# Linear attention's key transposes follow the values, empty steps between the gate pieces, and output tails at fixed steps of the last gate job and the first output job

## The chip, the cores and the metric

The program runs on one core of one Trainium2 chip. A run's time is device time in microseconds; the time of a kernel is the median of its runs. The engines of a core are PE (TensorE), DVE (VectorE), ACT (ScalarE), POOL (GpSimd) and SP (SyncE, which issues the weight transfers here). Each works through its own instructions in a fixed order, and waits where an operand or a buffer is not ready.

## The reference

Two layers of a 1024-wide hybrid block run over a sequence of 16 meta tokens and 512 frames (L = 528), followed by a second block of another kind, which the change does not touch. In each of the first block's layers one wide projection gives the inputs of two attentions: gated linear attention (4 heads) and forgetting attention (8 heads, softmax with a decay). Their normed and gated outputs lie side by side in `mix`, which the output projection multiplies. For the linear attention, cut to what the change touches:

```
log_b = cumsum(log_a)                       # per chunk of 64 frames, and for the meta tokens
u[c]  = sum_s (k_s * exp(log_end - log_b_s)) v_s^T
S_c   = exp(log_end) * S_{c-1} + u[c];   o_t = q_t^T S_c
mix   = concat(rms_norm(o) * silu(gate), fox) ;  h = h + mix @ w_out
```

Decays come from a low-rank projection (`sm`), through a log-sigmoid and a cumulative sum along the tokens.

## The kernel before

Activations stand transposed, 128 features on the partitions and 528 tokens along the row, each as a pair of rounded high and low halves. A projection onto 128 features is a job: 8 contraction tiles, for each of them three products (high by high, low by high, high by low) in two halves of 264 columns, so 48 matmuls on line 321 into a PSUM tile `mm`, of which there are two. When a job ends, DVE takes its `mm` tile out with a multiply by the row norm (`scaled`, L377, or L379 with a factor more); the next job but one cannot start before that. The weights of a job are split ahead of it: ACT rounds (`wh`, L272), DVE subtracts (`wl`, L273).

The order of jobs in a layer is a list: sm, gk0, gk1 (linear keys), fk0, fq0, fv0 (forgetting attention's first pair of heads: keys, queries, values), fk1, fq1, fv1, gv0, gv1 (linear values), then pairs 2 and 3 with gv2, gv3, gq0, gq1, then gr0 to gr3 (output gates), then 8 output jobs out0 to out7.

Everything that isn't a job is cut into pieces and put into a queue (`push`); while a job runs, after each of its 8 contraction tiles the queue hands out pieces at a rate (`pump`), a rate of 1.3 a step in the first jobs. A job can also carry pieces at fixed steps (`at`), and `flush` empties the queue before a job. A scheduler then sets the order on each engine; evacuations go with high priority, and `pin` holds an instruction to its place in the written order.

The pieces that the change concerns:

- `gates` (L383 on): the log-sigmoid of the decays, a scan along the tokens for the forgetting gate (`fox`, L417) and two sets of nine scans for the linear decays (`scan(0)`, `scan(1)`, L431), each followed on POOL by a subtraction (L434), on ACT by an exponential into `e` (L442) and small ones into `dec` (L449).
- `gla_k`: multiplies a key tile by `e` (L689), transposes it on PE (L693, L704) into PSUM tiles `to_tokensT`, of which there are two, and copies it out (L174, L176, L705) into zeroed tiles (L697). `gla_states` reads these much later, after gv3.
- `gla_v`: the same for the values (L462, L465).
- `fox_prep` (L519): transposes of fv0 as soon as it is out; `fox_k` (L492 to L494) and `stack_q` (L503) make high and low halves of keys and queries, the low ones on line 179.
- `gla_tail`: transposes of one head's normed output (L823, L827), two multiplies by gain and gate on DVE (L828), rounding on ACT (L829) and the low half on DVE (L179). It fills `mix[h]`. `st["scale"]` holds the multiplies by the head norm (L761) that go ahead of it.

In the kernel before, `gla_k` of a tile is pushed when that key job is taken out, and the tails of heads 0 and 1 and the scale pieces of heads 2 and 3 go through the queue when gr0 and gr1 are taken out; tails 2 and 3 stand at steps 2 and 4 of out0. The output jobs read `mix` in the order 4, 5, 6, 7, 0, 1, 2, 3.

Of the kernel before, what the change touches and what calls it, by code (L numbers as in the profile page):

```python
# [12 lines left out]
ALU = mybir.AluOpType  # L13
# [14 lines left out]
FULL = [(0, 264), (264, 264)]  # L28
# [8 lines left out]
class Net:  # L37
# [352 lines left out]
    def gates(self, i, sm, st):  # L390


        nc = self.nc
        R = slice(32, 40)
        ts, mzs = [self.G() for _ in range(3)], [self.G() for _ in range(3)]
        lbs, es, z = [], [], {}
        rows = [R, slice(0, 128), slice(0, 128)]

        def pre(m):
            bias = self.vec("ba", 2 * i + m)  # L400
            for a, n in ((0, HALF), (HALF, L - HALF)):
                ps = self.PS("gla_gateS_")
                nc.tensor.matmul(ps[:, :n], lhsT=self.wa[:, i, 128 * m:128 * m + 128], rhs=sm[:, a:a + n],
                                 start=True, stop=True)
                self.log_sigmoid_parts(ps[:, :n], bias, mzs[1 + m][:, a:a + n], ts[1 + m][:, a:a + n])

        def exps():
            for t, r in zip(ts, rows):
                nc.scalar.activation(t[r, :], t[r, :], AF.Exp, scale=-1.0)

        def logs():
            for t, r in zip(ts, rows):
                self.pin(nc.scalar.activation(t[r, :], t[r, :], AF.Ln, bias=1.0))

        def fox():
            c, z["r"] = self.G(), self.G()
            nc.vector.tensor_tensor_scan(c[R, :], mzs[0][R, :], ts[0][R, :], 0.0, op0=ALU.add, op1=ALU.subtract)  # L417
            nc.scalar.activation(self.c3[R, :], c[R, :], AF.Copy)
            nc.gpsimd.tensor_tensor(z["r"][R, :], c[R, :], self.c3[R, :], op=ALU.subtract)

        def fox_rest():
            r = z["r"]
            c2 = self.slots.tile([128, L], BF16, tag="g", name=self.n("g"))
            self.pin(nc.scalar.activation(c2[R, :], r[R, :], AF.Copy))
            self.pin(nc.scalar.activation(self.c3[0:8, :], r[R, :], AF.Copy))
            nc.gpsimd.tensor_tensor(self.c3[64:72, :], r[R, :], c2[R, :], op=ALU.subtract)

        def scan(m):
            lb, e, t, mz = self.G(), self.G(), ts[1 + m], mzs[1 + m]
            for a, n in [(0, META)] + [(META + 64 * c, 64) for c in range(8)]:  # L430
                nc.vector.tensor_tensor_scan(lb[:, a:a + n], mz[:, a:a + n], t[:, a:a + n], 0.0,  # L431
                                             op0=ALU.add, op1=ALU.subtract)
            lv = lb[:, META:].rearrange("p (c t) -> p c t", t=64)
            nc.gpsimd.tensor_tensor(e[:, META:].rearrange("p (c t) -> p c t", t=64), lv,  # L434
                                    lv[:, :, 63:64].to_broadcast([128, 8, 64]), op=ALU.subtract)
            nc.vector.tensor_scalar(e[:, :META], lb[:, :META], lb[:, META - 1:META], None, op0=ALU.subtract)
            lbs.append(lv)
            es.append(e)

        def decays():  # L440
            for m in range(2):
                nc.scalar.activation(es[m], es[m], AF.Exp, scale=-1.0 / 16)  # L442
                st["e"].append(es[m])
                for b in range(2):

                    dec = self.small.tile([128, 16], F32, tag=f"dec{2 * m + b}", bufs=2, name=self.n("dec"))
                    lv = lbs[m][64 * b:64 * b + 64].rearrange("p (j e) t -> p j e t", e=2)
                    for e in range(2):
                        nc.scalar.activation(dec[64 - 64 * e:128 - 64 * e, :4].unsqueeze(2), lv[:, :, e, 63:64],  # L449
                                             AF.Exp, scale=1.0 / 16)  # L450
                    st["dec"].append(dec)

        self.log_sigmoid_parts(sm[R, :], self.bf[R, i:i + 1], mzs[0][R, :], ts[0][R, :])
        return [lambda: pre(0), lambda: pre(1), exps, logs, fox, lambda: scan(0), lambda: scan(1), fox_rest, decays]

    def to_tokens(self, src, dst, dmeta, mcol, eng):

# [380 lines left out]
    def layer(self, i):  # L838
        nc, a = self.nc, self.a
        w_in = a["w_in"][i]  # L840
        st = dict(e=[], dec=[], kt=[], gvt=[], S={}, S0={}, om={}, on={}, gr={}, gk={}, gq={}, gv={}, scale={})
        fst = [dict() for _ in range(4)]
        mix = [None] * 8
# [27 lines left out]
        def ev_fk(p):  # L871
            return lambda ps: self.fox_k(fst[p], self.scaled(ps, FULL, self.rs))

        def ev_fq(p):
            def f(ps):
                t = self.scaled(ps, FULL, self.rs, extra=0.125)
                fst[p]["q"] = [self.stack_q(t, b) for b in range(2)]
            return f

        def ev_fv(p):  # L880
            def f(ps):
                fst[p]["fv"] = self.scaled(ps, FULL, self.rs)
                self.fox_pair(fst[p], i, p, mix, p == 3)
            return f

        def ev_gk(m):
            def f(ps):
                t = self.scaled(ps, FULL, self.rs)
                self.push(lambda: self.gla_k(st, m, t))
            return f  # L890

        def ev_gv(h):
            def f(ps):
                t = self.scaled(ps, FULL, self.rs)
                self.push(lambda: self.gla_v(st, h, t))
                if h == 3:
                    self.gla_states(st, 0)
                    self.gla_states(st, 1)
            return f
# [11 lines left out]
        def ev_gr(h):  # L911
            def f(ps):
                t = self.scaled(ps, FULL, self.rs)
                nc.scalar.activation(t, t, AF.Silu)
                tail = lambda: self.gla_tail(st, i, h, t, mix)
                if h == 0:
                    self.push(tail, *st["scale"][1])
                elif h == 1:
                    self.push(tail)
                else:  # L920
                    first_out["at"] = {**first_out.get("at", {}), 2 * h - 2: [tail]}
            return f

        rest = [(256, ev_gk(0)), (384, ev_gk(1))]
# [3 lines left out]
        for p in range(4):  # L928
            fox = [(2064 + 128 * p, ev_fk(p)), (1552 + 128 * p, ev_fq(p)), (2576 + 128 * p, ev_fv(p))]
# [9 lines left out]
                self.jobs[-2]["rate"] = 1.3  # L939

        self.norm_at(first, sums, spread)


        nxt = {}

        def ev_out(k):
            def f(ps):
                h = self.h[k]
                nc.vector.tensor_tensor(self.v(h, TO), self.psv(ps, TO), self.v(h, TO), op=ALU.add)
                if k == 0:  # L950
                    nxt["hs"] = []
                    nxt["acc"] = self.G()
                    if t0:
                        nc.gpsimd.memset(nxt["acc"][:, :t0], 1.0)
                nxt["hs"].append(self.hs_of(h[:, t0:], self.vec("ffn", 8 * i + k), None, t0, L))
                self.sq_acc(nxt["acc"], h[:, t0:], k == 0, 1.0, t0, L)
            return f
# [4 lines left out]
        for k in range(KT):  # L962
            if k % 2 == 0:
                ch = self.chunk([(self.wcols(w_out, 128 * k, 256), 0)], KT)
            self.job(ch, 128 * (k % 2), lambda: mix, TO, ev_out(k))
            if k == 0:
                first_out = self.jobs[-1]
            self.jobs[-1]["order"] = [4, 5, 6, 7, 0, 1, 2, 3]
            self.jobs[-1]["flush"] = k == 0

# [700 lines left out]
```

## Time and profile before

| | us |
|---|---|
| median of 3 runs | 2352.11 (2351.21 to 2354.13) |
| the profiled execution | 2356.24 |
| its span in the trace | 2354.5 |
| PE busy | 2316.9 (98% of the span) |
| DVE, ACT, POOL busy | 1369.2, 952.6, 251.8 (58%, 40%, 11%) |
| mean granted TensorE clock | 0.993 of full |
| chain that ended last, PE's share | 67% |

PE is busy nearly all the time, so what other engines do shows in the time only where PE stands, or where it runs at the lower of its two clocks. A row of the timeline gives the start, the duration, the engine, the line, the operation with output and input tiles, how many instructions of the kind were put together, and in brackets the idle time just before and what ended it.

### The profile page before, as it was taken

The page shows a single profiled execution, that of the slowest core. Times are in us where ns is not written, and L with a number is a line of the kernel's source. Part 1 is how long each engine was busy: PE and PEld are TensorE (multiplying, and loading weights), DVE is VectorE, ACT ScalarE, POOL GpSimd, SP SyncE. Part 2 cuts the span into 40 slices and gives each one's busy share as a digit, 9 for nine tenths or more (in the row PEclk, how much of TensorE's full clock was granted, in tenths as well). Part 3 has the DMA queues.
Part 4 walks back from the last instruction along what each step waited for, and adds up shares of the span by engine and source line. Part 5 has one row for each costly group of instructions (what it writes and reads, how often), then busy time and mean ns, then how long its engine had stood idle before and what let it go on. Part 6 is the DMA issues. An engine that isn't in the chain of part 4 may idle for free.

```text
span 2354.5 us, 37601 instructions
## 1 busy us (share of the span) xinstructions
PE 2316.9 (98%) x15703; PEld 2133.4 (91%) x15703; DVE 1369.2 (58%) x2445; ACT 952.6 (40%) x1641; POOL 251.8 (11%) x261
## 2 busy tenths in 40 slices
PE   7999999999999999999999999999999999999998
PEld 6999999999998998999998889988999888888888
DVE  6767556465556677466464666796454454333335
ACT  6565434233346655343242544322233533222225
POOL 3111210000022112200000131100000002101012
PEclk9999999999999999999999999999999999999999
DMA  4211122222332211222223222222212222332323
GB/s 115 73 55 55 55 90 90 90 90 88 96 87 55 55 55 55 90 91 90 90 84 106 82 80 87 90 90 90 90 54 72 72 90 90 95 102 90 99 85 130
DMA packets 217072, 196.77 MB, mean 84 GB/s; under 512 B 8987, under 2 KB 214791, under 8 KB 216903
## 3 DMA queue, kind: packets, MB, share of 16 engines
q1 hardware_dynamic: 216903, 194.37, 26.6%
q8 instruction: 124, 2.03, 0.3%
q14 instruction: 45, 0.37, 0.0%
HBM read 192.26 MB, written 2.10 MB: 83 GB/s over the span
## 4 chain that ended last, share of the span: by engine, by line
PE 67%; ACT 1%; DVE 1%; issue 1%; POOL 0%; DMA 0%; POOLq 0%; ACTq 0%; SPq 0%; DVEq 0%
PE mm L321 60%; PE valuesT L1157 1%; PE scoresS L1140 1%; PE foxV L619 1%; PE attend_pT L479 1%; PE foxT L599 0%; PE foxS L509 0%; ACT wh L272 0%; PE foxS L510 0%; PE spreadS L221 0%; DMA raw<-in_w_down_dram 0%; PE idx L509 0%; PE to_tokensT L462 0%; PE idx L510 0%; DVE g L431 0%
## 5 line engine op out<-in xcount | busy, mean ns | idle before, releaser
L321 PE MATMUL mm<-g,wh 128*128 128x264 f32 (+3 forms) x9168 | 1882.6, 316 | 9.5 <-DVE g L377 7.0
L321 PEld LDWEIGHTS mm<-g,wh 128*128 128x128 f32 x9168 | 1393.1, 190 | 109.0 <-issue 8.0
L321 PE MATMUL mm<-g,wl 128*128 128x264 f32 (+3 forms) x4552 | 1160.5, 313 | 0.0
L321 PEld LDWEIGHTS mm<-g,wl 128*128 128x128 f32 x4552 | 753.5, 190 | 49.6
L272 ACT ACTIVATE wh<-raw 128x1024 fp32r<-128x1024 f32 (+1 forms) x369 | 385.0, 1044 | 944.8 <-PE mm L321 800.6
L273 DVE TENSOR_TENSOR wl<-raw,wh 128x1024 fp32r<-128x1024 f32 (+1 forms) x369 | 444.1, 1204 | 74.8 <-ACT wh L272 65.9
L377 DVE TENSOR_TENSOR g<-mm,g 128x528 f32<-128x528 f32 (+2 forms) x228 | 158.5, 696 | 322.0 <-PE mm L321 317.3
L204 POOL TENSOR_TENSOR g<-g,g 128x528 f32<-128x528 f32 (+3 forms) x49 | 71.2, 1465 | 914.6 <-ACT g L203 568.1
L179 DVE TENSOR_TENSOR g<-g,g 128x512 fp32r<-128x512 f32 (+3 forms) x131 | 92.4, 706 | 38.4 <-ACT g L1009 29.2
L1034 DVE TENSOR_TENSOR g<-mm,g 128x528 f32<-128x528 f32 (+1 forms) x48 | 33.6, 700 | 119.1 <-PE mm L321 119.0
L991 ACT ACTIVATE g<-g,cv 128x528 f32<-128x528 f32 (+1 forms) x88 | 72.1, 819 | 17.7 <-DVE g L377 17.5
L1420 POOL TENSOR_TENSOR g<-g,g 128x512 f32<-128x512 f32 x22 | 38.9, 1767 | 281.9 <-ACT g L1419 281.9
L994 DVE SCALAR_TENSOR_TENSOR g<-g,cv,g 128x526 f32<-128x526 f32 (+1 forms) x88 | 66.8, 760 | 3.1
L993 DVE SCALAR_TENSOR_TENSOR g<-g,cv,g 128x527 f32<-128x527 f32 (+1 forms) x88 | 66.3, 754 | 1.8 <-ACT g L991 1.8
L179 DVE TENSOR_TENSOR g<-foxT,g 128x128 fp32r<-128x128 f32 (+1 forms) x160 | 50.5, 340 | 20.5 <-ACT g L604 18.2
L1005 ACT ACTIVATE g<-g 128x528 f32<-128x528 f32 (+1 forms) x44 | 28.1, 639 | 83.7 <-DVE g L994 83.7
L1007 DVE TENSOR_TENSOR g<-g,g 128x528 f32<-128x528 f32 (+1 forms) x44 | 30.8, 701 | 32.4 <-ACT g L1005 32.4
L187 POOL TENSOR_TENSOR sm<-sm,mhalf 128x10 f32<-128x10 f32 (+3 forms) x29 | 37.2, 1291 | 115.7 <-DVE sm L186 115.4
L574 ACT ACTIVATE g<-g,sm 128x144 f32<-128x144 f32 (+2 forms) x80 | 43.0, 538 | 16.0 <-DVE sm L570 15.3
L604 ACT ACTIVATE g<-foxT 128x256 fp32r<-128x256 f32 (+1 forms) x96 | 33.2, 346 | 27.9 <-PE foxT L599 21.8
L1009 ACT ACTIVATE g<-g 128x528 fp32r<-128x528 f32 (+1 forms) x44 | 28.1, 639 | 33.1 <-DVE g L1007 33.1
L1451 DVE TENSOR_TENSOR g<-mm,g 128x512 f32<-128x512 f32 x16 | 11.1, 692 | 50.0 <-PE mm L321 50.0
(282 smaller groups left out, 1696.4 us busy)
## 6 DMA issues: line engine op xcount, KB each, us to landing
raw<-in_w_up_dram SPq DMA_DIRECT2D x50, 1024.0 KB
raw<-in_w_in_dram SPq DMA_DIRECT2D x44, 1024.0 KB
raw<-in_w_down_dram SPq DMA_DIRECT2D x28, 896.0 KB
raw<-in_w_in_dram SPq DMA_DIRECT2D x28, 512.0 KB
raw<-in_w_out_dram SPq DMA_DIRECT2D x12, 1024.0 KB
raw<-in_w_down_dram SPq DMA_DIRECT2D x12, 1024.0 KB
raw<-in_w_gate_dram SPq DMA_DIRECT2D x10, 1024.0 KB
raw<-in_w_up_dram SPq DMA_DIRECT2D x10, 512.0 KB
```

What stands on the lines that cost most here:

```text
L179: (eng or self.nc.vector).tensor_tensor(out, x, hi.bitcast(F32), op=ALU.subtract)
L187: self.nc.gpsimd.tensor_tensor(out, v[:rows, :n], self.mhalf[:rows, :n], op=ALU.pow)
L204: nc.gpsimd.tensor_tensor(acc[:, t0:t1], tmp[:, t0:t1], acc[:, t0:t1], op=ALU.add)
L272: keep(nc.scalar.activation(hi[:, :K], src, AF.Copy))
L273: keep(nc.vector.tensor_tensor(lo[:, :K], src, hi[:, :K].bitcast(F32), op=ALU.subtract))
L321: nc.tensor.matmul(ps[:, b, :n], lhsT=w[:, k, :], rhs=x[:, t:t + n], start=(ki == 0 and pi == 0), stop=(ki == len(order) - 1 and pi == len ...
L377: self.nc.vector.tensor_tensor(self.v(out, toks), self.psv(ps, toks), self.v(rs, toks), op=ALU.mult)
L574: nc.scalar.activation(P[:qs, :N], P[:qs, :N], AF.Exp, scale=-1.0, bias=m, accum_out=col)
L991: nc.scalar.activation(A[:, lo:], U[:, lo:], AF.Identity, bias=self.vec("cb", 44 * i + t), scale=cw(2))
L993: nc.vector.scalar_tensor_tensor(A[:, s1:], U[:, s1 - 1:L - 1], cw(1), A[:, s1:], op0=ALU.mult, op1=ALU.add)
L994: nc.vector.scalar_tensor_tensor(A[:, s0:], U[:, s0 - 2:L - 2], cw(0), A[:, s0:], op0=ALU.mult, op1=ALU.add)
L1420: nc.gpsimd.tensor_tensor(z[:, META:], z[:, META:], self.rs[:, META:], op=ALU.mult)
```

## The change

Four things move; no arithmetic is added or taken away.

1. The transposes of the linear keys (`gla_k`) are pushed just ahead of those of the values with the same number, when gv0 and gv1 are taken out, and no longer when gk0 and gk1 are.
2. `gates` returns its pieces with empty steps between them (seven gaps), so that the queue hands out a scan later and spread out.
3. All the scans are pinned.
4. Tail 0 stands at step 1 of the last gate job (gr3), the two scale pieces at its steps 3 and 5, and tails 1, 2, 3 at steps 0, 2, 4 of out0.

```diff
@@ gates: scans
-            nc.vector.tensor_tensor_scan(c[R, :], mzs[0][R, :], ts[0][R, :], 0.0, op0=ALU.add, op1=ALU.subtract)
+            self.pin(nc.vector.tensor_tensor_scan(c[R, :], mzs[0][R, :], ts[0][R, :], 0.0, op0=ALU.add,
+                                                  op1=ALU.subtract))
...
-        return [lambda: pre(0), lambda: pre(1), exps, logs, fox, lambda: scan(0), lambda: scan(1), fox_rest, decays]
+        gap = lambda: None
+        return [lambda: pre(0), lambda: pre(1), exps, logs] + [gap] * 2 + [
+            fox, gap, lambda: scan(0), gap, gap, lambda: scan(1), gap, fox_rest, decays]
@@ layer: keys and values
         def ev_gk(m):
             def f(ps):
+                st["gk"][m] = self.scaled(ps, FULL, self.rs)
+            return f
+
+        def ev_gv(h):
+            def f(ps):
                 t = self.scaled(ps, FULL, self.rs)
-                self.push(lambda: self.gla_k(st, m, t))
-            return f
...
+                if h < 2:
+                    self.push(lambda: self.gla_k(st, h, st["gk"][h]))
                 self.push(lambda: self.gla_v(st, h, t))
@@ layer: gates of the output
                 nc.scalar.activation(t, t, AF.Silu)
-                tail = lambda: self.gla_tail(st, i, h, t, mix)
-                if h == 0:
-                    self.push(tail, *st["scale"][1])
-                elif h == 1:
-                    self.push(tail)
-                else:
-                    first_out["at"] = {**first_out.get("at", {}), 2 * h - 2: [tail]}
+                st["gr"][h] = t
...
+        tail = lambda h: lambda: self.gla_tail(st, i, h, st["gr"][h], mix)
+        scale = lambda x: lambda: st["scale"][1][x]()
+        self.jobs[-1]["at"] = {1: [tail(0)], 3: [scale(0)], 5: [scale(1)]}
...
             if k == 0:
-                first_out = self.jobs[-1]
+                self.jobs[-1]["at"] = {0: [tail(1)], 2: [tail(2)], 4: [tail(3)]}
```

In the changed file the lines behind `gates` stand three further down: the scan is L432, the multiply of a key L692, its transposes L696 and L707, a tail's multiplies L831.

**DVE in layer 0, behind the forgetting gate's scan.** Before, behind the first nine scans (g_449 is the key tile gk0, mm_466 is gk1's result, mm_612 fk0's):

```order
L431 SCALAR_TENSOR_TENSOR g_524<-g_445,g_442 128x64 x8
L436 TENSOR_SCALAR g_525<-g_524 128x16
L431 SCALAR_TENSOR_TENSOR g_543<-g_446,g_443 128x16
L431 SCALAR_TENSOR_TENSOR g_543<-g_446,g_443 128x64 x8
L436 TENSOR_SCALAR g_544<-g_543 128x16
L689 TENSOR_TENSOR g_449<-g_449,g_525 128x528
L273 TENSOR_TENSOR wl_609<-raw_451,wh_608 128x1024
L377 TENSOR_TENSOR g_603<-mm_466,g_381 128x528
L176 COPY g_592<-to_tokensT_587 64x4x64
L705 COPY km<-to_tokensT_600 16x2x64
L377 TENSOR_TENSOR g_678<-mm_612,g_381 128x528
L689 TENSOR_TENSOR g_603<-g_603,g_544 128x528
```

Of the change, from the end of the second nine scans to the evacuation of fv0 (mm_564 is fk0's result, mm_662 fq0's, mm_725 fv0's):

```order
L437 TENSOR_SCALAR g_578<-g_577 128x16
L692 TENSOR_TENSOR g_449<-g_449,g_537 128x528
L377 TENSOR_TENSOR g_644<-mm_564,g_381 128x528
L692 TENSOR_TENSOR g_555<-g_555,g_578 128x528
L179 TENSOR_TENSOR g_647<-g_644,g_646 64x528
L179 TENSOR_TENSOR g_653<-g_644,g_652 64x528
L273 TENSOR_TENSOR wl_659<-raw_451,wh_658 128x1024
L379 SCALAR_TENSOR_TENSOR g_711<-mm_662,g_381 128x528
L273 TENSOR_TENSOR wl_722<-raw_557,wh_721 128x1024
L179 TENSOR_TENSOR g_713<-g_711,g_713 64x528
L179 TENSOR_TENSOR g_716<-g_711,g_716 64x528
L377 TENSOR_TENSOR g_774<-mm_725,g_381 128x528
```

Ahead of that piece, between the two sets of scans, the change has gk1's evacuation (L377) and a weight split (L273). The copies L176 and L705 of the keys are gone from here; the multiplies of the keys by `e` have stayed.

**DVE around the first output job of layer 0.** Before, from the last weight split ahead of gr3 on (mm_3342 is gr2's result; the first L828 pair is tail 0's, the second tail 1's):

```order
L273 TENSOR_TENSOR wl_3442<-raw_2972,wh_3441 128x1024
L828 SCALAR_TENSOR_TENSOR g_3379<-gla_tailT_3380,cv,g_3170 128x272
L828 SCALAR_TENSOR_TENSOR g_3379<-gla_tailT_3385,cv,g_3170 128x256
L179 TENSOR_TENSOR g_3378<-g_3379,g_3377 128x528
L761 TENSOR_TENSOR g_3285<-g_3285,sm_3288 128x512
L761 TENSOR_TENSOR g_3315<-g_3315,sm_3318 128x512
L761 TENSOR_TENSOR om_3276<-om_3276,sm_3327 128x256
L828 SCALAR_TENSOR_TENSOR g_3408<-gla_tailT_3409,cv,g_3333 128x272
L828 SCALAR_TENSOR_TENSOR g_3408<-gla_tailT_3414,cv,g_3333 128x256
L273 TENSOR_TENSOR wl_3500<-raw_3336,wh_3499 128x1024
L179 TENSOR_TENSOR g_3407<-g_3408,g_3406 128x528
L377 TENSOR_TENSOR g_3438<-mm_3342,g_381 128x528
```

Of the change, from gr2's evacuation (mm_3342) on; mm_3414 is gr3's result, and L831 is tail 0 here:

```order
L377 TENSOR_TENSOR g_3407<-mm_3342,g_381 128x528
L186 TENSOR_SCALAR sm_3330<-sm_3326 128x2
L182 SCALAR_TENSOR_TENSOR g_3359<-foxN_3366,cv,g_3358 128x256
L273 TENSOR_TENSOR wl_3411<-raw_2972,wh_3410 128x1024
L831 SCALAR_TENSOR_TENSOR g_3423<-gla_tailT_3424,cv,g_3170 128x272
L831 SCALAR_TENSOR_TENSOR g_3423<-gla_tailT_3429,cv,g_3170 128x256
L179 TENSOR_TENSOR g_3422<-g_3423,g_3421 128x528
L764 TENSOR_TENSOR g_3285<-g_3285,sm_3288 128x512
L764 TENSOR_TENSOR g_3315<-g_3315,sm_3318 128x512
L377 TENSOR_TENSOR g_3480<-mm_3414,g_381 128x528
L764 TENSOR_TENSOR om_3276<-om_3276,sm_3327 128x256
L273 TENSOR_TENSOR wl_3486<-raw_3336,wh_3485 128x1024
```

gr2's evacuation has gone from behind tail 1 to ahead of tail 0. gr3's, which before came next to it, stands ahead of tail 1, whose three instructions follow directly behind the last row shown, in out0.

**PE in layer 0, in the job behind gv1, where values are transposed.** Before (g_1444 and g_1590 are the value tiles, mm_1802 the running job):

```order
L462 MATMUL to_tokensT_1765<-ident,g_1444 128x128 x4
L321 MATMUL mm_1802<-g_209,wl_1447 128x264
L321 MATMUL mm_1802<-g_226,wh_1446 128x264 x2
L321 MATMUL mm_1802<-g_227,wh_1446 128x264 x2
L321 MATMUL mm_1802<-g_226,wl_1447 128x264
L465 MATMUL to_tokensT_1771<-ident,g_1444 16x128
L462 MATMUL to_tokensT_1775<-ident,g_1590 128x128 x4
L465 MATMUL to_tokensT_1781<-ident,g_1590 16x128
```

Of the change (g_449 is the key tile gk0, g_1410 the first value tile, mm_1775 the running job):

```order
L696 MATMUL to_tokensT_1731<-ident,g_449 128x128 x4
L321 MATMUL mm_1775<-g_209,wl_1413 128x264
L321 MATMUL mm_1775<-g_226,wh_1412 128x264 x2
L321 MATMUL mm_1775<-g_227,wh_1412 128x264 x2
L321 MATMUL mm_1775<-g_226,wl_1413 128x264
L707 MATMUL to_tokensT_1744<-ident,g_449 16x128
L321 MATMUL mm_1775<-g_226,wl_1413 128x264
L321 MATMUL mm_1775<-g_244,wh_1412 128x264 x2
L321 MATMUL mm_1775<-g_245,wh_1412 128x264
L465 MATMUL to_tokensT_1748<-ident,g_1410 128x128 x4
L321 MATMUL mm_1775<-g_245,wh_1412 128x264
L468 MATMUL to_tokensT_1754<-ident,g_1410 16x128
```

Ahead of the values of head 0 now stand the five transposes of gk0, and behind these rows follow those of gk1 and of the second value tile in the same way. Before, the ten of the keys stood inside fk0 and fq0.

## Rows read from the trace of the kernel before

**Rows 1.** The page's first part: busy time and share of the span.

```profile
PE 2316.9 (98%) x15703; PEld 2133.4 (91%) x15703; DVE 1369.2 (58%) x2445; ACT 952.6 (40%) x1641; POOL 251.8 (11%) x261
```

**Rows 2.** Waits: engine and line, waited for; total us, times, longest.

```profile
PE to_tokensT L693 <- DVE g L689: 7.5, 3, 3.8
...
PE mm L321 <- DVE g L377: 7.0, 2, 3.5
```

**Rows 3.** Windows: us, busy (instructions) of PE, PEld, DVE, ACT, POOL; granted clock, DMA, GB/s.

```profile
50.20:56.90 6.70, 5.56 (x26) 5.49 (x27) 5.06 (x11) 4.88 (x12) 6.07 (x7) 0.50 0.00 0
...
57.10:63.80 6.70, 6.70 (x57) 6.68 (x57) 5.65 (x9) 3.53 (x7) 3.92 (x10) 1.00 0.42 128
...
130.00:140.00 10.00, 10.00 (x84) 9.75 (x83) 6.16 (x11) 6.95 (x12) 0.00 (x0) 1.00 0.41 107
...
258.50:265.10 6.60, 5.96 (x27) 6.00 (x28) 2.63 (x5) 1.90 (x3) 0.00 (x0) 0.50 0.01 2
...
729.50:732.70 3.20, 3.00 (x14) 2.69 (x13) 1.22 (x4) 2.12 (x7) 3.06 (x6) 0.50 0.00 0
...
937.70:940.90 3.20, 3.20 (x17) 3.20 (x16) 0.44 (x2) 0.61 (x1) 0.00 (x0) 0.50 0.00 0
```

**Rows 4.** Timeline of layer 0, from the start of fk0 to fq0.

```profile
43.03 0.64 PE L321 MATMUL mm<-g,wh 128*128 128x264 f32 x4
...
45.46 2.61 DVE L431 TENSOR_TENSOR_SCAN g<-g,g 128x16 f32<-128x16 f32 x9
...
48.12 2.44 DVE L431 TENSOR_TENSOR_SCAN g<-g,g 128x16 f32<-128x16 f32 x9
...
48.22 1.09 POOL L434 TENSOR_TENSOR g<-g 128x512 f32<-128x512 f32 x1 [0.84 <-DVE g L436]
...
50.63 2.69 POOL L434 TENSOR_TENSOR g<-g 128x512 f32<-128x512 f32 x1 [1.32 <-DVE g L431]
...
51.21 1.21 DVE L273 TENSOR_TENSOR wl<-raw,wh 128x1024 fp32r<-128x1024 f32 x1
...
51.34 1.12 PE L693 MATMUL to_tokensT<-ident,g 128*128 128x128 f32 x4 [3.75 <-DVE g L689]
...
53.36 0.64 ACT L442 ACTIVATE g<-g 128x528 f32<-128x528 f32 x1 [1.21 <-POOL g L434]
...
53.91 0.41 ACT L449 ACTIVATE dec<-g 64x4 f32<-64x4 f32 x2
...
54.91 1.06 ACT L272 ACTIVATE wh<-raw 128x1024 fp32r<-128x1024 f32 x1 [0.32 <-PE mm L321]
...
56.14 0.63 ACT L493 ACTIVATE g<-g 64x528 fp32r<-64x528 f32 x1
```

**Rows 5.** Timeline of layer 0: PE's first instructions of fk1, and fv0's transposes.

```profile
68.22 0.64 PE L321 MATMUL mm<-g,wh 128*128 128x264 f32 x4
...
69.19 0.65 PE L519 MATMUL foxV<-ident,g 128*128 128x128 f32 x4
```

**Rows 6.** Timeline of layer 0, around the start of out0.

```profile
251.14 0.88 DVE L828 SCALAR_TENSOR_TENSOR g<-gla_tailT,cv,g 128x272 f32<-128x272 f32 x2
...
257.67 0.70 DVE L179 TENSOR_TENSOR g<-g,g 128x528 fp32r<-128x528 f32 x1
...
258.29 1.31 DVE L377 TENSOR_TENSOR g<-mm,g 128x528 f32<-128x528 f32 x2
...
259.13 1.22 PE L321 MATMUL mm<-g,wh 128*128 128x264 f32 x4 [3.49 <-DVE g L377]
```

**Rows 7.** Timeline of layer 1: fk0's start, and the second scans.

```profile
722.32 0.73 PE L321 MATMUL mm<-g,wh 128*128 128x264 f32 x4 [0.33 <-DVE g L431]
...
724.73 2.44 DVE L431 TENSOR_TENSOR_SCAN g<-g,g 128x16 f32<-128x16 f32 x9
```

**Rows 8.** Timeline of DVE: the evacuations of out0 and out1 in layer 0.

```profile
269.12 0.71 DVE L949 TENSOR_TENSOR g<-mm,g 128x528 f32<-128x528 f32 x1 [0.85 <-PE mm L321]
...
274.96 0.71 DVE L949 TENSOR_TENSOR g<-mm,g 128x528 f32<-128x528 f32 x1 [3.03 <-PE mm L321]
```

More of the change, by code (lines that the diff above doesn't have):

```diff
@@ L430, in scan @@
             for a, n in [(0, META)] + [(META + 64 * c, 64) for c in range(8)]:
-                nc.vector.tensor_tensor_scan(lb[:, a:a + n], mz[:, a:a + n], t[:, a:a + n], 0.0,
-                                             op0=ALU.add, op1=ALU.subtract)
+                self.pin(nc.vector.tensor_tensor_scan(lb[:, a:a + n], mz[:, a:a + n], t[:, a:a + n], 0.0,
+                                                      op0=ALU.add, op1=ALU.subtract))
             lv = lb[:, META:].rearrange("p (c t) -> p c t", t=64)
@@ L887, in f @@
             def f(ps):
-                t = self.scaled(ps, FULL, self.rs)
-                self.push(lambda: self.gla_k(st, m, t))
+                st["gk"][m] = self.scaled(ps, FULL, self.rs)
             return f
```

## The prediction

> **What bounds the kernel now.** I read the page's busy times first: PE is busy for 98% of the span [rows 1]. So only two things can give time back: stretches in which PE stands, and stretches in which it runs at half clock. The list of waits comes next. Of PE's waits, two belong to code that the change touches [rows 2]: the key transposes (L693) waited three times for the multiply by `e` (L689), 7.5 us together, and a job's first matmul (L321) waited twice for an evacuation (L377), 7.0 us together. The timeline tells where. In layer 0 PE stands for 3.75 us at 51.34 until the key tile is multiplied [rows 4], and for 3.49 us at 259.13, where out0 starts, until gr2's `mm` tile is taken out [rows 6]. Layer 1 repeats both: 3.49 at out0, and 7.5 - 3.75 = 3.75 at its two key tiles. One small wait is added there, 0.33 us at 722.32 when fk0 wants its buffer [rows 7]. Together: 3.75 + 3.49 + 3.49 + 3.75 + 0.33 = 14.8 us of standing.
>
> The windows show the rest. From 50.2 to 56.9 the granted clock is 0.50 (1.2 GHz) and PE finishes 26 matmuls; in the 6.7 us behind it, at 1.00 (2.4 GHz), 57, so 0.1175 us each [rows 3]. At full clock 26 would take 3.05; PE was busy 5.56, so 2.5 us were lost to the clock. The stretch at out0 of layer 0 (5.96 busy, 27 matmuls) lost 2.8 by the same sum, those of layer 1 (3.00 busy with 14, 3.20 with 17) 1.35 and 1.2. Each of the four comes right behind one of the long waits, so I count them to the waits: 7.9 us. All that could be removed is 14.8 + 7.9 = 22.7 us.
>
> **The change, part by part.**
>
> *Output tails.* gr2's evacuation waited on DVE behind tail 1, whose two multiplies (0.88 for both) waited for PE transposes, and behind a weight split and a subtraction (0.70) [rows 6]. In the new order it stands ahead of tail 0, and gr3's ahead of tail 1. gr2's result is ready one whole job, 5.84 us (274.96 - 269.12, [rows 8]), before out0 wants the buffer, and only L182, a split and tail 0 lie around it. So both 3.49 go, with the clock losses 2.8 and 1.2: 11.0 us for both layers. What comes in is tail 1 in out0 beside tails 2 and 3. Each needs 0.88 + 0.70 us of DVE and a rounding on ACT of a tile like the one of 0.64 [rows 4] between them, 2.2 us in a row. Tail 3 starts at step 4 of 8, and contraction tile 3 comes last, at step 7, which is 3 x 0.73 = 2.2 us later. That is just enough when DVE is free, and DVE also has a split of 1.21 [rows 4] to do there. In the new order out1's first matmuls are mixed with out0's last 12, which covers most of a delay. I put 0.3 us a layer, between 0 and 1.5 (a split in front of the chain and 0.3).
>
> *The gates and keys of layer 0.* PE no longer transposes a key inside fk0, so the 3.75 and the 2.5 behind it go. The multiplies by `e` stay early on DVE, though, and with them the whole train behind the scans. I replay it from [rows 4] (jobs take 5.84, [rows 8]):
> - fk0 starts at 43.03, fq0 at 48.87, fv0 at 54.71, fk1 at 60.55. The first scans end at 48.07; gk1's evacuation follows at once (0.66, half of the pair at 258.29, [rows 6]), by 48.8, just in time for fq0.
> - A split (1.21) then goes ahead of the second scans (2.44), which end at 52.4 instead of 50.56.
> - POOL's subtraction for the second `e` follows. It took 1.09 beside scans and 2.69 beside a multiply, a split and an evacuation, 2.6 us of DVE work. Now only a multiply and an evacuation lie beside it: I take 1.75, with 2.69 as the upper end. It ends at 54.1, the exponential (0.64) at 54.8.
> - Behind that exponential on ACT stand the four copies of fk0's tile (0.63 each, to 57.3), two small exponentials (0.41) and the weight rounding (1.06), to 58.8. DVE's split waits for it: 60.0. Then in DVE's order: fq0's evacuation (0.66), a split (1.2), two subtractions (0.7 each, overlapping a little) and fv0's evacuation (0.66), to 63.8.
>
> Late next are the transposes of fv0. They stand 0.97 us into fk1 (69.19 against 68.22, [rows 5]), that is at 61.5; fv0's tile is there at 63.8. **So a new wait of 2.3 us comes in layer 0**, part of it perhaps 0.1 to 0.3 earlier, where fk1 wants fq0's buffer. With 2.69 for POOL everything is 0.94 later: 3.2. If the scheduler's train runs one split faster, 1.1; to 0 if ACT's four copies do not hold the rounding back. I take 2.3 and keep 0 to 3.5. The Trainium skill's "SBUF — State Buffer" (section "Who interferes with whom") says that a DVE instruction with two SBUF inputs contends with a GpSimd instruction that reads SBUF, and one with at most one SBUF input, as an evacuation has, does not. By that rule only the multiply would hold POOL, which gives 1.75 and the 2.3; by the row's full 2.69 the wait would be 3.2.
>
> A wait of 3.10 was followed by a half clock of 3.2 us that cost 1.35, one of 0.33 by none of its own [rows 2, 3, 7]. For 2.3 I take one such stretch, 1.3 us, between 0 and the 2.5 of [rows 3].
>
> *The same in layer 1.* All of 3.75 + 0.33 and the 1.35 go. Here gk0's evacuation is now ahead of the scans and both sets of scans stand ahead of gk1's. The second set started at 724.73 and took 2.44 [rows 7]; without the evacuation ahead of it (0.66) it ends at 726.5. Then a split (1.21) and gk1's evacuation (0.66): 728.4. fk0 started at 722.32 - 0.33 = 721.99 and, without a wait, ends at 727.83. fq0 waits 0.6 to 0.7 for its buffer: I take 0.7, between 0 and 1.9 (one more split). Later places have several us of slack, since fv0's rounding is not held by late scans.
>
> *The keys beside the values.* Ten transposes in each layer only change place on PE. In their old place they stood in fk0 and fq0, in the new one they share the two `to_tokensT` buffers with the ten of the values. That makes eight handovers a layer at which PE wants a buffer that ACT or DVE is still copying out. The stretch had PE busy for all of 10 us with ACT at 6.95 and DVE at 6.16 [rows 3], so copies queue for some tenths; the matmuls between the transposes cover most. I put 0.4 a layer, between 0 and 2. `gla_states` reads the keys behind gv3, several jobs later, so late copies delay nobody. POOL's memsets go with them; POOL did nothing in that stretch [rows 3]. SP's order is unchanged, and no transfer moves but with its job.
>
> *Pins and empty steps* cost no instruction; what they do is in the orders above.
>
> Sum: 22.7 - 2.3 - 1.3 - 0.7 - 0.8 - 0.6 = 17.0 us. The profiled execution took 2356.24, 1.7 more than its span and 4.1 more than the median 2352.11. It would become 2339.2; for the median I take off the same 17.0: **2335.1 us**.
>
> **The rivals.**
> - *No wait comes back.* ACT's copies run as early as their inputs, fv0 is out in time, and all 22.7 us are gained: 2329.4. The order speaks against it (rounding and split stand behind the copies on both engines), the uncertain POOL time for it. 12 in 100.
> - *The wait of the keys returns in full at fv0*, with 3.2 and the clock's 2.5 in layer 0, 1.9 and 1.3 in layer 1, 1.5 a layer in out0: 3.2 + 2.5 + 1.9 + 1.3 + 3.0 + 0.8 = 12.7, a gain of 10.0 us, 2342.1; with 2 us a layer at the handovers, 2345.3. For it: the same engines are as late as before, only the reader has changed. 9 in 100.
> - *The clock falls where keys and values are transposed together.* With one stretch of 1.3 us a layer the gain is 14.4: 2337.7. Against it: from 130 to 140 ten transposes ran beside matmuls with 1.00 granted [rows 3]. 4 in 100. The Trainium skill's "TensorE: Matmul & The Clock Gate" (Part 4, PE-mode transpose) states that transposes do not count as PE activity as matmuls do, which speaks for such a fall with twenty of them; the row at 1.00 does not bear it out for ten.
> - *Slower: the handovers of the two transpose buffers stall PE.* Sixteen of them, in both layers; at 1.1 us each (17.0 + 0.8 over 16) the gain is gone, from 1.4 each the kernel is slower by over 4.7. At 1.5 it would be 2358. For it: four copies on two engines must end before a key's buffer is free, and ACT has a rounding of 1.06 in its line. Against it: DVE and ACT idle a third of the stretch. 2 in 100.
> - *It does nothing.* gr2's evacuation is early in the order but late in time, and PE waits elsewhere for as long: within 4.7 us of before. 3 in 100.
>
> **How the numbers follow.** My forecast, as summed, has 70 in 100. The first four cases lie between 2329.4 and 2345.3. Leaving out the worse half of the second rival and the last two cases on one side, and only the edge of the first on the other, the range is 2328.5 to 2343. About 4.7 us (0.2%) is what a measurement of this kernel can tell from no change. Faster by more: 70 + 12 + 9 + 4 less 1 for sums at their worst, 0.94; within: 0.04; slower: 0.02.
>
> **What the profile of the changed kernel would show.** Right: no wait of the key transposes (now L696) and none of 3.49 before out0; full clock there; a wait of PE at the fv0 transposes of layer 0 (L522) of some 2 us, near 62, with a half clock behind it; 0.7 us of L321 on L377 near 728 less what was gained before it; full clock in the 10 us of key and value transposes. Wrong would be: waits of `to_tokensT` transposes on ACT or DVE copies above 1 us; out0 or out1 waiting for a low half (L179) of a tail; fk1 of layer 0 waiting for fq0's buffer by more than 1 us; or a half clock in a stretch that had none.

## The result, and the profile after

The changed kernel took 2337.71 us (median of 6 runs, 2335.06 to 2338.46) against 2354.7 (median of 6, 2351.21 to 2355.94): a ratio of 0.9926 (the ratios in this text are not quotients of the two medians), 95% interval 0.9916 to 0.9936, 17.0 us less. Two later rounds gave 2336.55 against 2355.06 (chip 3: 0.9922, 0.991 to 0.9935) and 2337.28 against 2354.88 (chip 2: 0.9931, 0.9919 to 0.9944). The forecast was 17.0 us off the median then at hand, 2335.1.

The profiled execution has a span of 2336.7 us where that of before has 2354.5, 17.8 less. The page's busy times, to lay beside [rows 1]:

```profile
PE 2311.3 (99%) x15703; PEld 2126.2 (91%) x15703; DVE 1369.9 (59%) x2445; ACT 953.3 (41%) x1641; POOL 254.4 (11%) x261
```

The other engines do the same work as before. PE does the same number of instructions in 5.6 us less busy time, which goes with the clock (see the account below), and the rest of the 17.8 is standing time. The waits of PE that were at stake, to lay beside [rows 2] (total us, times, longest):

```profile
PE foxV L522 <- DVE g L377: 2.2, 3, 1.9
...
PE mm L321 <- DVE g L377: 0.7, 1, 0.7
```

The wait for the key multiply has gone from the list, and so have the two of 3.49. What has come in is one wait of 1.86 us at fv0's transposes in layer 0 and one of 0.75 at the start of fq0 in layer 1:

```profile
718.90 0.73 PE L321 MATMUL mm<-g,wh 128*128 128x264 f32 x4 [0.75 <-DVE g L377]
```

The timeline of layer 0 shows the train that makes the first of them; it answers to [rows 4]:

```profile
48.14 0.70 DVE L377 TENSOR_TENSOR g<-mm,g 128x528 f32<-128x528 f32 x1
48.76 1.62 DVE L273 TENSOR_TENSOR wl<-raw,wh 128x1024 fp32r<-128x1024 f32 x1
50.30 1.64 DVE L432 TENSOR_TENSOR_SCAN g<-g,g 128x16 f32<-128x16 f32 x9
52.02 1.56 POOL L435 TENSOR_TENSOR g<-g 128x512 f32<-128x512 f32 x1 [2.73 <-DVE g L432]
53.61 0.65 ACT L443 ACTIVATE g<-g 128x528 f32<-128x528 f32 x1
54.29 1.73 DVE L692 TENSOR_TENSOR g<-g,g 128x528 f32<-128x528 f32 x1 [0.99 <-ACT g L443]
56.14 0.65 ACT L497 ACTIVATE g<-g 64x528 fp32r<-64x528 f32 x1
57.25 2.01 ACT L272 ACTIVATE wh<-raw 128x1024 fp32r<-128x1024 f32 x2
58.34 1.23 DVE L273 TENSOR_TENSOR wl<-raw,wh 128x1024 fp32r<-128x1024 f32 x1 [0.88 <-ACT wh L272]
59.48 0.70 DVE L379 SCALAR_TENSOR_TENSOR g<-mm,g 128x528 f32<-128x528 f32 x1
61.35 1.61 DVE L179 TENSOR_TENSOR g<-g,g 64x528 fp32r<-64x528 f32 x2
62.99 0.71 DVE L377 TENSOR_TENSOR g<-mm,g 128x528 f32<-128x528 f32 x1
63.76 0.91 PE L522 MATMUL foxV<-ident,g 128*128 128x128 f32 x4 [1.86 <-DVE g L377]
```

The reader should follow it downward: each row starts about where the one that it needs, or the one ahead of it on its engine, ends. gk1 is taken out by 48.84, and fq0 starts at 48.99 with no wait in the list. The second scans end at 51.9, POOL's subtraction at 53.6, the exponential at 54.3, ACT's four copies at 56.8. Only then does ACT round the next weights, DVE split them, and DVE reach fv0's tile at 62.99.

The windows answer to [rows 3] (us, then busy time and instructions of PE, PEld, DVE, ACT, POOL, granted clock, DMA share, GB/s):

```profile
49.20:52.50 3.30, 3.30 (x29) 3.30 (x29) 3.30 (x12) 1.51 (x5) 0.57 (x2) 1.00 0.00 0
61.80:63.80 2.00, 0.14 (x2) 0.05 (x1) 1.94 (x4) 0.81 (x1) 0.60 (x1) 1.00 1.04 362
64.10:67.30 3.20, 3.20 (x16) 2.94 (x15) 1.89 (x5) 1.53 (x5) 0.00 (x0) 0.50 0.43 106
67.50:70.70 3.20, 3.20 (x27) 2.77 (x25) 1.26 (x7) 1.74 (x7) 0.00 (x0) 1.00 0.82 216
126.00:136.00 10.00, 9.95 (x80) 9.19 (x79) 6.81 (x15) 6.71 (x13) 0.00 (x0) 1.00 0.41 107
244.00:250.50 6.50, 6.50 (x56) 6.50 (x55) 6.08 (x15) 2.13 (x4) 3.13 (x3) 1.00 0.02 4
```

From 49.2 to 52.5, where PE before stood until 51.34 and then ran at 0.50, it is busy throughout at 1.00. Behind the new wait PE has one stretch at 0.50 (1.2 GHz) and does 16 instructions in 3.2 us there, against 27 in the next 3.2: (27 - 16) x 3.2 / 27 = 1.3 us lost, an estimate, since the two stretches do not hold the same instructions. Where keys and values are transposed together (126 to 136) PE is busy for 9.95 of 10 us at 1.00.

Around out0, DVE takes out gr2 (first row), gr3 (second), and multiplies tail 1 (third). To lay beside [rows 6]:

```profile
246.99 0.70 DVE L377 TENSOR_TENSOR g<-mm,g 128x528 f32<-128x528 f32 x1
...
252.62 0.70 DVE L377 TENSOR_TENSOR g<-mm,g 128x528 f32<-128x528 f32 x1
...
254.71 0.89 DVE L831 SCALAR_TENSOR_TENSOR g<-gla_tailT,cv,g 128x272 f32<-128x272 f32 x2
```

Before, both evacuations stood together behind tail 1. Now gr2 is out 5.6 us ahead of gr3, and PE has no idle stretch of 0.1 us or more between 247 and 262.

### The profile page after: what moved, and what is told of

Read it like the earlier page. It is cut to its first block, busy times and chain, and to the rows that moved or that the text cites. A ratio compares the mean times of both kernels' runs of the same rounds, so it can differ in the third digit from the quotient of the medians.

```text
span 2336.7 us, 37580 instructions
## 1 busy us (share of the span) xinstructions
PE 2311.3 (99%) x15703; PEld 2126.2 (91%) x15703; DVE 1369.9 (59%) x2445; ACT 953.3 (41%) x1641; POOL 254.4 (11%) x261
## 4 chain that ended last, share of the span: by engine, by line
PE 67%; ACT 1%; DVE 1%; issue 1%; DMA 0%; POOL 0%; POOLq 0%; ACTq 0%; SPq 0%; DVEq 0%
PE mm L321 60%; PE valuesT L1160 1%; PE scoresS L1143 1%; PE foxV L622 1%; PE attend_pT L482 1%; PE foxT L602 0%; PE foxS L512 0%; PE foxS L513 0%; DMA raw<-in_w_down_dram 0%; PE idx L512 0%; ACT wh L272 0%; PE spreadS L221 0%; PE idx L513 0%; DVE g L432 0%; PE token_sumsT L210 0%
## 5 line engine op out<-in xcount | busy, mean ns | idle before, releaser
L321 PE MATMUL mm<-g,wh 128*128 128x264 f32 (+3 forms) x9168 | 1879.0, 315 | 3.1 <-ACT wh L272 1.4
L321 PEld LDWEIGHTS mm<-g,wh 128*128 128x128 f32 x9168 | 1388.2, 189 | 103.7 <-ACT wh L272 1.7
L321 PE MATMUL mm<-g,wl 128*128 128x264 f32 (+3 forms) x4552 | 1160.0, 313 | 0.0
L321 PEld LDWEIGHTS mm<-g,wl 128*128 128x128 f32 x4552 | 750.5, 189 | 50.4
L273 DVE TENSOR_TENSOR wl<-raw,wh 128x1024 fp32r<-128x1024 f32 (+1 forms) x369 | 444.9, 1206 | 74.6 <-ACT wh L272 64.2
L377 DVE TENSOR_TENSOR g<-mm,g 128x528 f32<-128x528 f32 (+2 forms) x228 | 158.7, 696 | 319.7 <-PE mm L321 315.1
```

Of the source, the lines that this page charges most:

```text
L273: keep(nc.vector.tensor_tensor(lo[:, :K], src, hi[:, :K].bitcast(F32), op=ALU.subtract))
L321: nc.tensor.matmul(ps[:, b, :n], lhsT=w[:, k, :], rhs=x[:, t:t + n], start=(ki == 0 and pi == 0), stop=(ki == len(order) - 1 and pi == len ...
L377: self.nc.vector.tensor_tensor(self.v(out, toks), self.psv(ps, toks), self.v(rs, toks), op=ALU.mult)
```

## Experiments

### One part at a time: the tails

The kernel before, with only the fourth part of the change: the tails and scale pieces at fixed steps.

```diff
-                    self.push(tail, *st["scale"][1])
...
+        self.jobs[-1]["at"] = {1: [tail(0)], 3: [scale(0)], 5: [scale(1)]}
...
+                self.jobs[-1]["at"] = {0: [tail(1)], 2: [tail(2)], 4: [tail(3)]}
```

> The kernel before with only the output tails moved (tail 0 and the scale pieces into gr3, tails 1 to 3 into out0); gates and keys as before. Theory of separate waits: both waits of 3.49 us ahead of out0 and the half clocks behind them (2.8 and 1.2 us) go, nothing comes in, so 11.0 us less than before, some 2343; the waits of 3.75 and 3.10 at the key transposes stay to a tenth. Rival, the waits come back inside out0, where tail 1 now lies beside tails 2 and 3: waits of 1 us and more at a job in out0 or out1 and a gain of 8 us or less.

Measured: 2343.37 against 2354.06, ratio 0.9957 (0.9941 to 0.9972), 10.7 us less. No wait of a job's start (L321) for an evacuation (L377) is left in the list, and no new one stands in it; the one for the key multiply stays:

```profile
PE to_tokensT L693 <- DVE g L689: 7.4, 3, 3.8
```

So the tails are worth what was summed for them, and tail 1 in out0 brings no wait in.

### One part at a time: gates and keys

The changed kernel with the tails put back (the diff above, the other way round).

> The changed kernel with the output tails put back as before; gates with empty steps and keys beside the values stay. Theory of separate waits: 6 to 7 us less than before, 2347 to 2348, with the new waits of 1.9 us at fv0's transposes in layer 0 and 0.75 in layer 1, and with 3.49 us twice ahead of out0 and half clock behind it. Rival, the parts lean on each other (the tails gain more or less when the gates come earlier): this kernel's gain and that of the tails alone do not add up to the 17 to 18 us of the whole, by 2 us or more.

Measured: 2348.84 against 2354.06, ratio 0.9976 (0.9966 to 0.9985), 5.2 us less. The waits:

```profile
PE mm L321 <- DVE g L377: 7.7, 3, 3.5
```

That is 3.48 and 3.49 ahead of out0 and 0.68 in layer 1. The time gained is a little under the 6 to 7 expected. 10.7 + 5.2 = 15.9, against 17.0 to 18.5 for the whole in three rounds, so the parts come out 1.1 to 2.6 us short, and the line of 2 us that was drawn ahead lies inside that. Their waits do add up: each kernel lacks the waits of its own part and keeps those of the other. The single runs of this kernel lie between 2345.3 and 2351.15 with granted clocks from 0.998 to 0.995, so a shortfall of that size is within what goes with the clock. Whether the parts lean on each other by 2 us or so is not shown.

### Without the empty steps

```diff
-        gap = lambda: None
-        return [lambda: pre(0), lambda: pre(1), exps, logs] + [gap] * 2 + [
-            fox, gap, lambda: scan(0), gap, gap, lambda: scan(1), gap, fox_rest, decays]
+        return [lambda: pre(0), lambda: pre(1), exps, logs, fox, lambda: scan(0), lambda: scan(1), fox_rest, decays]
```

As the diff shows, the empty steps are six in a layer, not seven.

> The changed kernel without the empty steps in the gates (scans still pinned, keys beside the values, tails moved). In its order gk1's evacuation stands on DVE behind both sets of scans and a weight split again. Theory: it ends at 45.5 + 2.6 + 2.4 + 0.2 + 1.2 + 0.7 = 52.4 instead of 48.8, and fq0 of layer 0 wants the buffer at 48.9: a wait of some 3.4 us there, with 1.3 to 2.5 us of half clock, while the wait at fv0 (1.9) and its half clock (1.3) go because PE comes later; layer 1 has about 0.3 + 0.4 us more. So 2 to 4 us slower than the changed kernel, a gain of 13.5 to 15.5 on before. Rival, the empty steps do nothing once the keys have left: the same time as the changed kernel, no wait at fq0.

Measured: 2339.08, ratio 0.9936 (0.9919 to 0.9952). The timeline of layer 0:

```profile
48.16 2.44 DVE L432 TENSOR_TENSOR_SCAN g<-g,g 128x16 f32<-128x16 f32 x9
...
51.77 0.70 DVE L377 TENSOR_TENSOR g<-mm,g 128x528 f32<-128x528 f32 x1
...
52.62 0.71 PE L321 MATMUL mm<-g,wh 128*128 128x264 f32 x4 [3.54 <-DVE g L377]
```

gk1's evacuation ends at 52.47 and fq0 waits for it by 3.54 us, where 52.4 and some 3.4 were forecast; the wait at fv0 is gone, because PE now comes later. Behind the wait at fq0 lies one half-clock stretch (53.7 to 57.1). The time is 1.4 to 2.5 us above the changed kernel's three medians, which the intervals alone do not separate; the wait does. So in layer 0 moving the keys without the empty steps only moves the wait from the key transposes to the next job's buffer. In layer 1 it does more: the 3.10 and 0.61 us at the key transposes go, and 0.78 at fq0 comes in. That is why this kernel is still 4.3 us faster than the tails alone on the same chip. The pins do nothing: without them the order of every engine is row for row that of the change, so that version was not run.

### Keys in their old place

The changed kernel with `gla_k` pushed when gk0 and gk1 are taken out.

```diff
-                st["gk"][m] = self.scaled(ps, FULL, self.rs)
+                t = self.scaled(ps, FULL, self.rs)
+                self.push(lambda: self.gla_k(st, m, t))
...
-                if h < 2:
-                    self.push(lambda: self.gla_k(st, h, st["gk"][h]))
```

> The changed kernel with the keys' transposes pushed in their old place (behind gk0 and gk1); empty steps and tails as in the change. In its order PE transposes gk0 two matmuls into fq0 of layer 0, at 49.1, and the tile is multiplied by 52.7. Theory: PE waits 3.6 us there and about 1.5 more at gk1 in fq0, half clock behind it (2.5), so of layer 0's 6.2 us nothing is gained; in layer 1 some 3 us likewise. The time is that of the tails alone within 2 us, a gain of 9 to 12. Rival, the empty steps alone take the keys' wait away: a gain of 15 and more.

Measured: 2343.28, ratio 0.9952 (0.9937 to 0.9967): the time of the tails alone. PE's timeline in layer 0, and the granted clock in layers 0 and 1:

```profile
52.79 0.65 PE L696 MATMUL to_tokensT<-ident,g 128*128 128x128 f32 x4 [3.25 <-DVE g L692]
56.08 0.63 PE L696 MATMUL to_tokensT<-ident,g 128*128 128x128 f32 x4 [1.31 <-DVE g L692]
```

```profile
56.10:62.80 6.70, 6.40 (x52) 6.19 (x53) 6.08 (x11) 4.83 (x9) 5.57 (x12) 1.00 0.50 152
720.00:723.20 3.20, 3.09 (x15) 3.01 (x16) 2.28 (x5) 1.75 (x7) 3.08 (x6) 0.50 0.00 0
```

The waits are there, 4.6 us in layer 0 and 3.74 in layer 1. The half clock is there in layer 1, from 719.9 to 723.3. In layer 0 it is not: after standing for 3.25 and 1.31 us PE goes on at 1.00. The trace is of the fastest of this kernel's four runs. So the empty steps without the moved keys gain nothing (0.1 us on the tails alone), the moved keys without the empty steps 4.3; and in layer 0 each alone leaves PE waiting for what the scans hold back.

### The changed kernel once more

No edit; what is asked is whether the waits and the half clocks come again.

> The changed kernel once more, on one chip with the three kernels that follow. Theory: the waits (1.86 at fv0's transposes in layer 0, 0.75 at fq0 in layer 1) are those of the first trace to a tenth, since the order sets them; the half clocks are not tied to one wait and lie elsewhere or are fewer or more in this execution, each worth 1.2 to 1.4 us. Rival: the same half clocks at the same places, one behind the wait at fv0 and two behind the norms.

Measured: 2336.55, ratio 0.9922 (0.991 to 0.9935).

```profile
62.95 0.66 PE L522 MATMUL foxV<-ident,g 128*128 128x128 f32 x4 [1.86 <-DVE g L377]
```

```profile
60.90:63.10 2.20, 0.34 (x3) 0.15 (x2) 2.14 (x4) 0.91 (x1) 0.69 (x1) 1.00 1.09 376
63.20:66.40 3.20, 3.20 (x26) 2.80 (x24) 2.19 (x6) 2.16 (x8) 0.00 (x0) 1.00 0.42 92
```

The wait is 1.86 to the hundredth, and this time PE runs at 1.00 behind it; the half clocks at the two norms came back. A third time, beside the last experiment below, the wait was 1.86 and the half clock was there again:

> The changed kernel beside it, for a comparison on one chip: 2335 to 2338, with the waits of 1.86 and 0.75 as in both traces before, and half clocks in one to three places.

```profile
63.70:66.90 3.20, 3.20 (x16) 2.94 (x14) 1.66 (x5) 1.53 (x5) 0.00 (x0) 0.50 0.48 113
```

The two waits were the same in all three, 1.86 and 0.73 to 0.75. Whether the clock falls behind it differs from one execution to the next of the same kernel.

### fv0's transposes later

```diff
+        if p == 0 and i == 0:
+            self.push(*[lambda: None] * 3)
         self.push(lambda: self.fox_prep(st, p), lambda: self.fox_gates(st, p))
```

> The changed kernel with three empty steps ahead of fv0's transposes in layer 0, which puts them 24 matmuls into fk1 instead of 8, some 1.9 us later. Theory: the wait of 1.86 falls to 0.1 or less and no wait takes its place, so 1.8 us, and up to 1.3 more when the half clock behind it goes: 1.5 to 3.2 us faster than the changed kernel. Rival, the scores and the pieces behind are late by the same amount and PE waits later in fk1 or at the start of fq1: the same time as the changed kernel.

Measured: 2334.68, ratio 0.9912 (0.9899 to 0.9926), 1.9 us below the changed kernel on the same chip. The longest wait at L522 is 0.2 us now (1.9 before), and no other takes its place; the 0.7 in layer 1 stays.

```profile
PE foxV L522 <- DVE g L377: 0.3, 2, 0.2
```

### The subtraction of e on DVE

```diff
-            nc.gpsimd.tensor_tensor(e[:, META:].rearrange("p (c t) -> p c t", t=64), lv,
+            nc.vector.tensor_tensor(e[:, META:].rearrange("p (c t) -> p c t", t=64), lv,
```

> The changed kernel with the two subtractions of e (L435) on DVE in place of POOL, in each layer. Theory of the train: fv0's tile is late because the second subtraction (1.56 on POOL), the exponential and ACT's four copies of fk0 stand one behind the other ahead of a weight rounding. On DVE the subtraction takes some 0.7, the scheduler puts that rounding ahead of the copies, and DVE and POOL no longer share SBUF reads there; fv0's evacuation ends at 61.5 to 62.2 instead of 63.7 and the wait falls from 1.86 to 0 to 0.6. Faster than the changed kernel by 1.3 to 3.2 us (with the half clock). Rival, DVE's load is the bound: with 1.4 us more on DVE the wait at fv0 grows to 2.5 or more, and gk1's evacuation at 48.8 is late by 0.7.

Measured: 2335.64 (2332.74 to 2338.65), ratio 0.9919 (0.9907 to 0.9932), 0.9 below the changed kernel on the same chip, which the runs do not tell from nothing. Neither theory had all of it:

```profile
PE foxV L522 <- DVE g L377: 1.3, 3, 0.9
...
PE mm L321 <- DVE g L377: 0.5, 1, 0.5
```

The wait at fv0 fell by 0.93, from 1.86 to 0.93, where the train's theory gave 1.3 to 1.9, and gk1's evacuation became late by 0.54, where the rival had 0.7. The rival's other half, a longer wait at fv0, did not come. The second scans took 2.61 us here (from 49.95), beside POOL's subtraction of 51.22, against 1.64 in the changed kernel, so this train was 1.0 us longer there, and fv0's evacuation ended at 62.84, where the theory had 61.5 to 62.2. With four more empty steps between the scans of layer 1:

> The kernel with e on DVE and, in layer 1, four more empty steps between the two sets of scans, so that gk1's evacuation stands between them there as in layer 0. Theory: the wait of 0.75 (with the subtraction on DVE about 1.4) at fq0 of layer 1 goes as well, and nothing else changes: 0.7 to 1.5 us faster than the kernel with e on DVE, 2 to 4.5 us faster than the changed kernel. Rival: the second scans are late then, and PE waits at fv0 of layer 1 by 1 us or more.

Measured: 2334.62, ratio 0.9913 (0.99 to 0.9927). The two waits of layer 0 stay at 0.55 and 0.90. The wait that these steps were to remove was not there to be removed: with e on DVE the scheduler already puts gk1's evacuation of layer 1 ahead of the weight split, and no wait of 0.2 us or more at that layer's fq0 is left in either kernel. So the 1.0 us between the two medians is not that of a removed wait, and the 2 to 4.5 us expected against the changed kernel came out as 1.9.

### Both new waits taken away

The changed kernel with the three empty steps ahead of fv0's transposes in layer 0 (their diff stands above) and four more between the scans of layer 1:

```diff
-            fox, gap, lambda: scan(0), gap, gap, lambda: scan(1), gap, fox_rest, decays]
+            fox, gap, lambda: scan(0)] + [gap] * (2 + 4 * i) + [lambda: scan(1), gap, fox_rest, decays]
```

> The changed kernel with both of its new waits taken away and POOL's work left where it is: three empty steps ahead of fv0's transposes in layer 0, and four more between the two sets of scans in layer 1. Theory: the wait of 1.86 goes as it did with the first edit alone, the one of 0.75 goes since gk1's evacuation stands between the scans, so 2.6 us less than the changed kernel's 2336.6 on the earlier chip, some 2334 (before at about 2355), by which a ratio of 0.990 to 0.991; half clocks move single runs by 1.3 each. Rival: the later second scans of layer 1 make PE wait at fv0 or fk0 there by 0.7 or more, and nothing is gained over the first edit alone.

Measured: 2333.58 (2332.85 to 2335.58), ratio 0.9917 (0.9904 to 0.9931), against 2337.28 of the changed kernel on the same chip (0.9931). DVE in layer 1:

```profile
711.47 0.70 DVE L377 TENSOR_TENSOR g<-mm,g 128x528 f32<-128x528 f32 x1
713.26 1.23 DVE L273 TENSOR_TENSOR wl<-raw,wh 128x1024 fp32r<-128x1024 f32 x1 [1.09 <-ACT wh L272]
714.40 1.64 DVE L432 TENSOR_TENSOR_SCAN g<-g,g 128x16 f32<-128x16 f32 x9
```

gk1 is out before the second scans, and none of PE's waits for L377 of 0.3 us or more is left in the two layers. It is 3.7 us of median below the changed kernel, of which 2.6 are the two waits; the rest goes with the granted clock, 0.998 in the profiled execution against 0.997, with one half-clock stretch of 3.4 us against three. That it beats the kernel with fv0 later alone is not shown: it is 21.3 us of median below the kernel before on its chip at a ratio of 0.9917, the other 20.4 on its own at 0.9912. That the second wait is gone stands in the trace.

## Why the prediction was right

**What could be removed.** The waits of [rows 2, 7] went as listed: of 14.8 us, 14.8 are gone from their places, and 1.86 + 0.75 = 2.6 have come in. The net is 12.2 us, where the forecast had 14.8 less 2.3, 0.7, 0.8 and 0.6, so 10.4.

**Tails.** Right, by the kernel with the tails alone: 10.7 us against 11.0. The 0.3 us a layer for tail 1 in out0 was too much; there was none.

**Layer 0's new wait.** Right in place and size: 1.86 at fv0's transposes against 2.3. The replay of the train was 0.5 us late from the second scans to the exponential: the second scans took 1.64, not 2.44, and POOL's subtraction 1.56, not 1.75. Two other terms gave part of that back: the split ahead of the scans took 1.62 instead of 1.21, the two subtractions ahead of fv0 1.61 instead of 1.4. In all, fv0's tile was out at 63.70 against 63.8. Most of the 0.4 between 2.3 and 1.86 lies on PE's side: fk1 began at 60.77, not 60.55, and the profile counts the wait from the end of its last matmul ahead of the transposes, at 61.90, where the replay had 61.5. That the train sets the wait, and not DVE's load, is shown halfway: with the subtraction on DVE the wait halved, and DVE's extra load made a new one of 0.54. How much of the train is owed to ACT's four copies standing ahead of the weight rounding was not tested by itself. That PE need not wait anywhere when fv0's transposes stand later is shown by the kernel with the later transposes.

**Layer 1.** 0.75 against 0.7, at fq0 as forecast.

**Keys beside the values.** Their 0.4 us a layer are not to be seen: PE was busy for 9.95 of 10 us there, and no wait of these transposes of 0.2 us or more stands in the list. The clock did not fall there either: with twenty transposes among the matmuls of these 10 us it stayed at 1.00. The Trainium skill's "TensorE: Matmul & The Clock Gate" (Part 4, PE-mode transpose) states that transposes do not count as matmuls do; no run here shows it.

**The clock.** The size was right and the reason too simple. The step "Each of the four comes right behind one of the long waits, so I count them to the waits" holds as a mean only. Before, up to the end of PE's work, the trace has six half-clock places: two of 6.8 us and two of 3.4 behind the four long waits [rows 3], and two of 3.4 at norms. After, it has three of 3.4, one behind fv0's wait and two at norms. The places at norms, two of the kernel before and two of the changed one:

```profile
705.60:708.80 3.20, 3.20 (x17) 3.20 (x16) 1.23 (x1) 0.96 (x1) 1.09 (x2) 0.50 0.29 71
1374.60:1377.80 3.20, 3.20 (x9) 2.52 (x8) 1.39 (x2) 1.06 (x1) 1.17 (x1) 0.50 0.00 0
```

```profile
695.60:698.80 3.20, 3.20 (x17) 3.20 (x16) 1.22 (x1) 1.06 (x1) 1.44 (x2) 0.50 0.44 109
1354.40:1357.60 3.20, 3.20 (x9) 2.45 (x9) 1.19 (x4) 1.06 (x1) 1.17 (x1) 0.50 0.00 0
```

A place of 6.8 counts as two stretches of 3.4, so there are five stretches less. At 1.3 us each they are 6.5 us, close to the 7.9 - 1.3 = 6.6 that were summed, and somewhat more than the 5.6 by which PE's busy time fell. But with the keys in their old place 3.25 and 1.31 us of standing in layer 0 brought none, and the same wait of 1.86 brought one in two executions of the changed kernel out of three. The kernel before itself runs from 2350.45 at a mean clock of 0.996 to 2357.15 at 0.993.

That the median moved by 17.0, the very sum, is partly chance: 1.8 us more of standing went than forecast, and the other two rounds gave 18.5 and 17.6. Of the signs of being wrong that the prediction named, none is in the trace.

## What to carry to other kernels

When a wait is removed by moving its reader, ask what else hangs on the late engine and replay its queue from the last event that does not move: here the first scans still end when they did (48.1), the second later (51.9 against 50.6), and the next buffer (fq0) or the next reader (fv0) inherits the wait unless an evacuation is put between the pieces. Empty steps in a work queue are a cheap way to let an urgent evacuation pass, and worth trying one wait at a time; here they gained nothing while the late reader stayed in its place. Count standing time from the order, and half clock only as a mean over executions.

## What the runs showed of the hardware

Two things were not expected.

The granted clock behind a wait is not a property of the wait: see the three traces of the changed kernel, and the 3.25 us of standing in layer 0 that were followed by 1.00. A long wait still made a half clock likely. Over the traces of all runs, ten of the eleven waits of 3.1 to 3.8 us brought one (four of 6.8 us, six of 3.4). The wait of 1.86 brought one in two of the three traces of the changed kernel, and in that of the kernel with the old tails. None of the waits of 0.5 to 0.93 at a job's start or at fv0 did.

DVE and POOL slow each other more widely than the prediction allowed for. The nine scans took 2.61 and 2.44 us before [rows 4]; POOL's subtraction of 46.18 (1.20 us, line 419) ran beside the first set and that of 48.22 beside the second. They took 1.64 where no POOL instruction ran (50.30 in layer 0 and 714.40 in the last kernel). For the rest, here are rows of the changed kernel, then of the last kernel, where the key multiply is L694:

```profile
51.98 0.70 DVE L692 TENSOR_TENSOR g<-g,g 128x528 f32<-128x528 f32 x1
54.25 1.20 POOL L427 TENSOR_TENSOR c<-g,g 8x528 bf16<-8x528 f32 x1
```

```profile
711.60 1.04 POOL L435 TENSOR_TENSOR g<-g 128x512 f32<-128x512 f32 x1 [0.87 <-DVE g L437]
716.09 0.70 DVE L694 TENSOR_TENSOR g<-g,g 128x528 f32<-128x528 f32 x1
716.12 1.56 POOL L435 TENSOR_TENSOR g<-g 128x512 f32<-128x512 f32 x1 [3.48 <-DVE g L432]
```

The multiply took 0.70 at 51.98, where it started just ahead of POOL's subtraction (52.02), and 1.73 at 54.29, just behind POOL's subtraction of 54.25. So of these two the one that started first kept its length. POOL's subtraction for `e` took 1.04 with only an evacuation beside it (711.47 and 711.60), 1.56 with one multiply beside it (716.09 and 716.12), the same 1.56 with the multiply and an evacuation (52.02), and 2.69 when a weight split came as well [rows 4]. The evacuation, which has one SBUF input, therefore adds nothing. The prediction's 1.75 for a multiply and an evacuation was 0.2 too long, its upper end of 2.69 did not apply. This agrees with the Trainium skill's "SBUF — State Buffer" (Who interferes with whom), which names DVE instructions with two SBUF inputs against GpSimd's reads.
